# An encoder layer on one core: the first up tile's order, splits moved from GpSimd to VectorE, exponentials and inverse roots kept in PSUM, deeper gate loads

## The chip, the core and the metric

The kernel runs on one core of a Trainium2 chip. A core has five engines with a queue of instructions each: TensorE (PE, matrix products into PSUM), VectorE (DVE), ScalarE (ACT), GpSimd (POOL) and SyncE (SP, which here only issues DMA transfers; ACT issues some too). Data lies in SBUF (128 partitions) or in PSUM (banks of 128x512 fp32), and the engines wait for one another by semaphores. The metric is the device time of one execution in microseconds; lower is better. A change of less than about 0.2% can't be told from none.

## The reference

One layer of an encoder with a final norm, for 1024 prompt tokens and 256 sample tokens that share the weights, all in fp32:

```
h = rmsnorm(x);  proj = h @ w_in      # q,k,v, beta/decay inputs, gates, gMLP u/v, two branch gates
y_a = deltanet(q,k,v,...) @ w_up_a    # 4 heads, two directions, chunks with a triangular inverse
y_b = (gelu(u) * (w_s @ layernorm(gelu(v)) + b)) @ w_up_b
x  += (sigmoid(gate_a)*y_a + sigmoid(gate_b)*y_b) @ w_out
x  += softmax(q k^T) v @ w_o          # 4 heads, 256 memory tokens, q from rmsnorm(x), k/v from rmsnorm(mem)
gu  = rmsnorm(x) @ w_gate_up          # 1024 -> 2 x 2816
x  += (silu(gate) * up) @ w_down
y   = rmsnorm(x)
```

## The kernel before

**Precision.** Each fp32 operand of a large product is split into two parts: `hi`, its rounding to the fast matmul type (an ACT pass), and `lo`, the rest (a subtraction on DVE or POOL); a product is three matmuls, hi.hi, lo.hi and hi.lo. `split(hi, lo, src, eng)` (L125, L126) does both, and `eng` says who subtracts.

**Blocks.** The tokens stand as columns in three blocks, b = 0 and 1 of 512 and b = 2, the sample, of 256; the channels as 8 tiles of 128 rows. The order of stages: first norm, sv/u projections and the gMLP; q/k/v and gates with the DeltaNet heads 0 to 3 and a batch of the sample's four heads beside them; the memory projections `mem_k` and `mem_v` (770 to 880 us); the branch projections `up_b` and `up_a` (to 1040); w_out, attention, w_o; the FFN's up half (1450 to 2040) and its down half with the final norm.

**Order.** PE's order is written out by hand. Main generators issue matmuls and advance a modelled clock by their cost; side generators (norms, DeltaNet batches, loads) are resumed when that clock passes the number that they yielded, so numbers such as `ROOT`, `LAGF` and `PACEF` set where a side's instructions fall between the main ones. The other engines' order follows from the program order and a scheduler. `K.take()` returns the split of the next weight tile in a fixed list, `K.ahead()` splits the one after and requests the next load (raw weights, two buffers); with `K.lo_vector` true DVE does the subtraction of these weights, else POOL.

**Norms.** `Norm.add` squares a tile on ACT and sums on DVE (or POOL); `Norm.rest` sums over the partitions with matmuls against a column of ones (`nacc`), takes the inverse square root on DVE (`rsqrt`, an integer start at L224 and three rounds of L226, L227, L228 on tiny tiles, `nst`), spreads it with matmuls against the identity (`nst`), and scales the tiles (`nt`, L275; with `shared`, some on ACT and POOL, L270, L271).

**Memory stage.** While PE does `mem_k`, DVE computes the sample batch's triangular inverse (`W`, L721 and L724, row by row) and the end of head 3: the output `o` is scaled by an inverse root (`cw`) at L920, and PE transposes it (L121). `yb`, `ylo` are the splits of the branch inputs, `stage` and `ga`/`gb` tiles hold stored gates (`gtd`, `tbd`) that are loaded back.

**Attention.** Per chunk of 128 tokens DVE takes the negative maximum of a score bank (L1277), ACT the exponential into `e` with its sum (L1279), DVE the scaling (L1281); PE transposes `e`.

**FFN up.** The gate and up products of a tile `f` are formed from seven half products (a scheme of Strassen's kind) of the left inputs b11, b21, b22, r1, r2, t3, t4; `gate_of` and `times_up` combine the banks `pb`, `pf`, `pe`, `pa` (pool `pm`, four banks). r2, t3 and t4 of the first tile are built by DVE at the stage's start, t3 and t4 ahead of the generator's first matmul in program order. `pn` and `pn2` belong to the next tile.

Of the kernel before, what the change touches and what calls it, by code (L numbers as in the profile page):

```python
# [8 lines left out]
F32 = mybir.dt.float32  # L9
F32R = mybir.dt.float32r  # L10
# [153 lines left out]
def trunk_kernel(ctx: ExitStack, tc: tile.TileContext, a):  # L164
# [65 lines left out]
    class Norm:  # L230
# [16 lines left out]
        def rest(self, xk, wcol, sink, pace=1300, shared=(), lag=1500, ks=range(KT), inplace=False, ready=None):  # L247
# [5 lines left out]
            for c in range(nb):  # L253
                mm(pc[:, c : c + 1], self.acc[:, c * P : (c + 1) * P], one)
            st = p.tile([P, 3, 4], F32, tag="nst", name="nst", bufs=2)
            ms, y, sc = (st[:, i, :nb] for i in range(3))
# [74 lines left out]
    def sv_load(half):  # L331
        lo = svp.tile([P, 8 * 264], F32R, tag="lo", name="svl")
        hi = svp.tile([P, 8 * 264], F32R, tag="hi", name="svh")
        for i in range(2):
            sl = slice(i * 1056, (i + 1) * 1056)
            raw = K.raw()
            SY.dma_start(raw, a["w_sv"][half][:, sl])
            split(hi[:, sl], lo[:, sl], raw, V if half and i else G)
# [7 lines left out]
    SY.dma_start(cst, a["const"])  # L346
    x_h = act_tiles()
    first = K.side(norm(xp, lambda k: xs[:, k, :], NS, S_MIX, to_h(x_h, 2), 0, 0))
    sv_load(0)
    x0 = x_load(a["xT"], 0, 512, "x0")  # L350
    sv_load(1)
# [641 lines left out]
    K.lo_vector = False  # L993
# [24 lines left out]
    def load_yb():  # L1018
        for b, (t0, n) in enumerate(BLOCKS):
            hi, lo = yb_h[b]  # L1020
            for k in range(4):
                raw = staging(n)
                SY.dma_start(raw, ybd[k, :, t0 : t0 + n])
                split(hi[:, k, :], lo[:, k, :], raw, G)
                yield 2000

    def mem_k(m):
        w = K.take()
        ps = bank(pm)
        for k in range(KT):  # L1030
# [5 lines left out]
            if k == 3:  # L1036
                K.ahead()
# [4 lines left out]
    def mem_v(h):  # L1042
        pss = [bank(pm)[:, :256] for _ in range(4)]
        for i in range(2):
            w = K.take()
            for c in range(4):
# [7 lines left out]
                if c == 1:  # L1054
                    K.ahead()
# [37 lines left out]
    def load_ya():  # L1093
# [14 lines left out]
        def finish(b, k, t):  # L1108
            hi, lo = y_h[b]
            V.tensor_tensor(out=t[0], in0=t[0], in1=t[1], op=ALU.mult)  # L1110
            split(hi[:, k : k + 2, :], lo[:, k : k + 2, :], t[0], V if b else G)
# [35 lines left out]
    def merge_load():  # L1147
        if len(merged) < len(jobs):
            m, b = jobs[len(merged)]
            t0, n = BLOCKS[b]  # L1150
            ta, tb = (up.tile([P, 512], F32, tag=f"g{x}", name=f"g{x}", bufs=3)[:, :n] for x in "ab")
# [4 lines left out]
    def up_a():  # L1156
        merge_load()
# [14 lines left out]
    K.main(up_a())  # L1172
    ues.close()
# [4 lines left out]
    class OutProj:  # L1178
# [21 lines left out]
        def run(self, xsrc, scale, wcol, xpool, store, sinks=None, then=None, ready=None):  # L1200
# [23 lines left out]
            for b, (t0, n) in enumerate(BLOCKS):  # L1224
# [17 lines left out]
                else:  # L1242
                    norm_b = nms[b].rest(xk, wcol, sinks(b, x, hs), 600, inplace=True)
# [18 lines left out]
    def attend(h, qh, ql, kh, kl, vh, vl, o_h):  # L1262
        es = {}

        def scores(b, c):
# [13 lines left out]
            S.activation(e, ps, AF.Exp, bias=st[:, 0:1], accum_out=st[:, 1:2])  # L1279
            V.reciprocal(st[:, 2:3], st[:, 1:2])  # L1280
            V.tensor_scalar(out=e, in0=e, scalar1=st[:, 2:3], scalar2=None, op0=ALU.mult)  # L1281
# [215 lines left out]
    split(*gu_w[0, 2], gu_raw[0][0], V)  # L1497
# [3 lines left out]

    for k in range(4):
        parts(r2, k, r2_raw[k], V)
    for k in range(4):
        V.tensor_tensor(out=x1[:, k, :], in0=x1[:, k + 4, :], in1=x1[:, k, :], op=ALU.subtract)
        parts(t3, k, x1[:, k, :], V)
    xhs.close()
    fs = ExitStack()
    fp = fs.enter_context(pool("ffn", side="right"))
# [294 lines left out]
```

## Time and profile before

| | us |
|---|---|
| median of 3 runs (2341.19 to 2343.51) | 2341.20 |
| the profiled execution | 2346.75 |
| its span, first to last instruction | 2344.8 |
| busy in it: PE / DVE / ACT / POOL | 2245.1 / 1320.2 / 754.6 / 660.3 |
| mean granted TensorE clock | 0.986 |

In the rows of the timeline the columns are the start in us, the duration in us, the engine, the line of the program, the operation and `out<-in` with shapes; `x4` says that neighbouring rows were joined, and the bracket gives the engine's idle time before the row and what ended it. In a table of stretches each engine's busy time in the stretch stands with its number of instructions, then the granted clock, the busy share of the DMA engines and GB/s. A row of waits gives the total of one kind of wait, the number, and the longest.

### The profile page before, as it was taken

To read this page: it belongs to the slowest core of one execution; us is meant where nothing else is said; L and a number is where in the kernel's file an instruction comes from. 1 tells how busy PE (TensorE), PEld (TensorE's weight loads), DVE (VectorE), ACT (ScalarE), POOL (GpSimd) and SP (SyncE) were. 2 spreads that over 40 slices of the span, in tenths; PEclk is the share of its full clock that TensorE was granted. 3 is DMA by queue.
4 is the path that set the end of the run, shared out by engine and by line. 5 is a ranking of instruction groups with operands and counts; after the bars stand their busy time and mean duration, and the time that the engine had idled before them with its cause. 6 is when DMAs were issued, how large, how long until landed. Compare 5 with 4: busy or idle time off the path is not lost. (4 is left out here: it accounts for less than half of the span.)

```text
span 2344.8 us, 32531 instructions
## 1 busy us (share of the span) xinstructions
PE 2245.1 (96%) x12592; PEld 1952.6 (83%) x12592; DVE 1320.2 (56%) x2716; ACT 754.6 (32%) x1391; POOL 660.3 (28%) x409
## 2 busy tenths in 40 slices
PE   5999999999999899999999999899999999999997
PEld 4988888888888788878888888788888888888886
DVE  7758688887967844464534547522322323656445
ACT  4433242433423433122234423332222223312113
POOL 3010000000001522123221321666666665212114
PEclk9999999999999999999999999999999999999998
DMA  4221312223243535763221431121211221723202
GB/s 147 102 86 65 113 53 91 76 66 89 65 133 94 164 107 203 236 227 115 74 93 59 156 132 63 67 87 66 69 62 66 78 72 44 255 99 102 81 10 90
DMA packets 170309, 237.83 MB, mean 101 GB/s; under 512 B 71386, under 2 KB 98858, under 8 KB 170154
## 3 DMA queue, kind: packets, MB, share of 16 engines
q1 hardware_dynamic: 150314, 206.65, 27.3%
q10 hardware_dynamic: 19840, 29.11, 3.4%
q8 instruction: 98, 1.61, 0.3%
q14 instruction: 57, 0.47, 0.1%
HBM read 166.20 MB, written 69.51 MB: 101 GB/s over the span
## 5 line engine op out<-in xcount | busy, mean ns | idle before, releaser
L108 PE MATMUL bank<-hi,whi 128*128 128x512 f32 (+1 forms) x2144 | 766.4, 357 | 10.7 <-DVE g L1548 8.8
L108 PE MATMUL bank<-hi,wlo 128*128 128x512 f32 (+1 forms) x2144 | 750.1, 350 | 0.0
L108 PE MATMUL bank<-lo,whi 128*128 128x512 f32 (+1 forms) x2144 | 750.1, 350 | 0.0
L108 PEld LDWEIGHTS bank<-hi,whi 128*128 128x128 f32 x2144 | 407.3, 190 | 60.6 <-issue 9.6
L108 PEld LDWEIGHTS bank<-hi,wlo 128*128 128x128 f32 x2144 | 406.4, 190 | 54.3
L108 PEld LDWEIGHTS bank<-lo,whi 128*128 128x128 f32 x2144 | 407.7, 190 | 48.5 <-issue 0.2
L126 POOL TENSOR_TENSOR wlo<-raw,whi 128x1024 fp32r<-128x1024 f32 x97 | 244.8, 2526 | 584.9 <-ACT whi L125 537.6
L125 ACT ACTIVATE whi<-raw 128x1024 fp32r<-128x1024 f32 x151 | 159.2, 1058 | 355.8 <-PE bank L108 275.3
L108 PE MATMUL bank<-ghi,whi 128*128 128x512 f32 (+1 forms) x528 | 189.3, 358 | 1.2 <-DVE x L1682 1.2
L108 PE MATMUL bank<-ghi,wlo 128*128 128x512 f32 (+1 forms) x528 | 188.5, 357 | 0.8 <-DVE wlo L126 0.8
L108 PE MATMUL bank<-glo,whi 128*128 128x512 f32 (+1 forms) x528 | 187.4, 355 | 0.0
L1682 DVE SCALAR_TENSOR_TENSOR x<-bank,x 128x512 f32<-128x512 f32 (+1 forms) x192 | 112.5, 598 | 132.6 <-PE bank L108 126.4
L126 POOL TENSOR_TENSOR wlo<-room,whi 128x1024 fp32r<-128x1024 f32 x42 | 101.7, 2422 | 126.7 <-ACT whi L125 126.7
L108 PEld LDWEIGHTS bank<-ghi,whi 128*128 128x128 f32 x528 | 99.4, 188 | 17.0 <-DVE x L1682 2.1
L108 PEld LDWEIGHTS bank<-ghi,wlo 128*128 128x128 f32 x528 | 99.3, 188 | 16.6 <-DVE wlo L126 1.3
L108 PEld LDWEIGHTS bank<-glo,whi 128*128 128x128 f32 x528 | 99.5, 188 | 15.1
L126 POOL TENSOR_TENSOR glo<-graw,ghi 128x1280 fp32r<-128x1280 f32 x13 | 46.4, 3588 | 203.3 <-ACT ghi L125 203.3
L1645 DVE TENSOR_TENSOR room<-room,bank 128x512 f32<-128x512 f32 x21 | 14.4, 688 | 143.0 <-ACT room L1528 143.0
L721 DVE TENSOR_TENSOR W<-W,UT 128x2 f32<-128x2 f32 (+30 forms) x155 | 84.7, 546 | 14.3 <-DMA W<-in_eye 9.5
L125 ACT ACTIVATE whi<-room 128x1024 fp32r<-128x1024 f32 x42 | 44.6, 1061 | 137.3 <-PE bank L108 137.3
L575 DVE SCALAR_TENSOR_TENSOR acc<-craw,sm,acc 128x510 f32<-128x510 f32 (+1 forms) x96 | 72.5, 756 | 23.1 <-ACT acc L573 22.0
L1548 DVE TENSOR_TENSOR g<-room,bank 128x512 f32<-128x512 f32 x42 | 28.9, 687 | 97.5 <-PE bank L108 97.5
(303 smaller groups left out, 3875.0 us busy)
## 6 DMA issues: line engine op xcount, KB each, us to landing
raw<-in_w_gu SPq DMA_DIRECT2D x44, 512.0 KB, 3.8
graw<-gd SPq DMA_DIRECT2D x20, 640.0 KB, 5.3
gd<-t SPq DMA_DIRECT2D x44, 256.0 KB, 2.4
raw<-in_w_dn SPq DMA_DIRECT2D x22, 512.0 KB, 4.0
raw<-in_w_g SPq DMA_DIRECT2D x20, 512.0 KB, 3.4
gtd<-gs ACTq DMA_DIRECT2D x32, 256.0 KB, 2.0
raw<-in_w_qkv SPq DMA_DIRECT2D x12, 512.0 KB, 3.6
x<-in_xT SPq DMA_DIRECT2D x10, 512.0 KB, 8.7
```

The source lines that it names most:

```text
L108: self.nc.tensor.matmul(out, l, r, start=start, stop=stop, skip_group_check=more)
L125: self.nc.scalar.activation(hi, src, AF.Copy)
L126: (eng or self.nc.vector).tensor_tensor(out=lo, in0=src, in1=f32(hi), op=ALU.subtract)
L575: V.scalar_tensor_tensor(out=dst, in0=src, scalar=wj, in1=dst, op0=ALU.mult, op1=ALU.add)
L721: V.tensor_tensor(out=t3, in0=u3[:, i:, c:].rearrange("p j c -> p c j"), in1=XL[:, 32 * i + i : 32 * i + 32].unsqueeze(1).to_broadcast([P, ...
L1548: V.tensor_tensor(out=g, in0=p, in1=ps, op=ALU.add)
L1645: V.tensor_tensor(out=c22, in0=u3, in1=pe, op=ALU.add)
L1682: V.scalar_tensor_tensor(out=x2[b][:, m, :], in0=ps, scalar=0.5, in1=x2[b][:, m, :], op0=ALU.mult, op1=ALU.add)
```

## The change

Eight edits, which the diff shows in the order of the file:

1. `rsqrt` in a norm works in the norm's PSUM bank (columns 4 to 11) rather than in SBUF; only its result lies in SBUF.
2. At the start, the first norm squares pairs of tiles (512 columns) and sums both halves with the matmuls; the constants are loaded in two parts around the first two sv weights; of each sv half DVE splits the second part.
3. `K.lo_vector` stays true through the memory and branch projections, and the yb and ylo splits go to DVE: no split of these stages is left on POOL. `K.ahead()` comes at the first step of a tile rather than the fourth or second.
4. `ROOT` for head 3 goes from 10000 to 16000, which moves the transposes of `o` 27 rows later in PE's order.
5. `up_a` loads its gates three jobs ahead, in six buffers, rather than one ahead in three.
6. The exponential stays in its PSUM bank and is scaled from there.
7. The first up tile: t3 and t4 are made inside the generator, behind the first matmul groups; `pn2` stands ahead of the t3 product; the next tile's raw weights are loaded in two parts at two places; the norm of block 1 has a slower pace (`PACE1`).
8. The final norm: lags 3500, 2800 and 1500 for the blocks in place of 4500, pace 500 in place of 700, and the sums of tiles from `FADD` on are on DVE (6 and 4 rather than 8 and 8; block 2's were there).

```diff
-        def rest(self, xk, wcol, sink, pace=1300, shared=(), lag=1500, ks=range(KT), inplace=False, ready=None):
+        def rest(self, xk, wcol, sink, pace=1300, shared=(), lag=1500, ks=range(KT), inplace=False, ready=None, halves=1):
...
-                mm(pc[:, c : c + 1], self.acc[:, c * P : (c + 1) * P], one)
-            st = p.tile([P, 3, 4], F32, tag="nst", name="nst", bufs=2)
-            ms, y, sc = (st[:, i, :nb] for i in range(3))
+                for i in range(halves):
+                    mm(pc[:, c : c + 1], self.acc[:, i * n + c * P : i * n + (c + 1) * P], one, i == 0, i == halves - 1)
+            y = p.tile([P, 4], F32, tag="nst", name="nst", bufs=2)[:, :nb]
+            ms, sc = pc[:, 4 : 4 + nb], pc[:, 8 : 8 + nb]
...
-    def sv_load(half):
+    def sv_raw(half):
+        raws = [K.raw() for _ in range(2)]
+        for i, raw in enumerate(raws):
+            SY.dma_start(raw, a["w_sv"][half][:, i * 1056 : (i + 1) * 1056])
+        return raws
+    def sv_split(half, raws):
...
-        for i in range(2):
+        for i, raw in enumerate(raws):
...
-            raw = K.raw()
-            SY.dma_start(raw, a["w_sv"][half][:, sl])
-            split(hi[:, sl], lo[:, sl], raw, V if half and i else G)
+            split(hi[:, sl], lo[:, sl], raw, V if i else G)
...
-    SY.dma_start(cst, a["const"])
+    SY.dma_start(cst[:, C_BD:], a["const"][:, C_BD:])
+    sv_raw0 = sv_raw(0)
+    SY.dma_start(cst[:, :C_BD], a["const"][:, :C_BD])
...
-    first = K.side(norm(xp, lambda k: xs[:, k, :], NS, S_MIX, to_h(x_h, 2), 0, 0))
-    sv_load(0)
+    def first_norm():
+        nm = Norm(xp, 512)
+        for k in range(0, KT, 2):
+            nm.add(xs[:, k : k + 2, :].rearrange("p k t -> p (k t)"))
+        nm.n = NS
+        yield from nm.rest(lambda k: xs[:, k, :], S_MIX, to_h(x_h, 2), 0, lag=0, halves=2)
+    first = K.side(first_norm())
+    sv_split(0, sv_raw0)
...
-    sv_load(1)
+    sv_split(1, sv_raw(1))
...
-    K.lo_vector = False
...
-                split(hi[:, k, :], lo[:, k, :], raw, G)
+                split(hi[:, k, :], lo[:, k, :], raw, V)
...
-            if k == 3:
+            if k == 0:
...
-                if c == 1:
+                if c == 0:
...
-            split(hi[:, k : k + 2, :], lo[:, k : k + 2, :], t[0], V if b else G)
+            split(hi[:, k : k + 2, :], lo[:, k : k + 2, :], t[0], V)
...
-            ta, tb = (up.tile([P, 512], F32, tag=f"g{x}", name=f"g{x}", bufs=3)[:, :n] for x in "ab")
+            ta, tb = (up.tile([P, 512], F32, tag=f"g{x}", name=f"g{x}", bufs=6)[:, :n] for x in "ab")
...
-        merge_load()
+        for _ in range(3):
+            merge_load()
...
+    K.lo_vector = False
...
-                    norm_b = nms[b].rest(xk, wcol, sinks(b, x, hs), 600, inplace=True)
+                    norm_b = nms[b].rest(xk, wcol, sinks(b, x, hs), (600, PACE1)[b], inplace=True)
...
-            S.activation(e, ps, AF.Exp, bias=st[:, 0:1], accum_out=st[:, 1:2])
+            S.activation(ps, ps, AF.Exp, bias=st[:, 0:1], accum_out=st[:, 1:2])
...
-            V.tensor_scalar(out=e, in0=e, scalar1=st[:, 2:3], scalar2=None, op0=ALU.mult)
+            V.tensor_scalar(out=e, in0=ps, scalar1=st[:, 2:3], scalar2=None, op0=ALU.mult)
...
-    split(*gu_w[0, 2], gu_raw[0][0], V)
...
+    split(*gu_w[0, 2], gu_raw[0][0], V)
...
-    for k in range(4):
-        V.tensor_tensor(out=x1[:, k, :], in0=x1[:, k + 4, :], in1=x1[:, k, :], op=ALU.subtract)
-        parts(t3, k, x1[:, k, :], V)
-    xhs.close()
...
-    fp = fs.enter_context(pool("ffn", side="right"))
-    t4 = [fp.tile([P, 4, 512], F32R, tag=f"t4{i}", name=f"t4{i}") for i in "hl"]
-    for k in range(4):
-        V.scalar_tensor_tensor(out=x0[:, k + 4, :], in0=r2_raw[k], scalar=-1.0, in1=x0[:, k + 4, :], op0=ALU.mult, op1=ALU.subtract)
-        parts(t4, k, x0[:, k + 4, :], V)
-    split(*gu_w[0, 3], gu_raw[0][1], V)
-    room = x0p.tile([P, KT, 512], F32, tag="x0", name="room")
+    t4 = []
+    def make_t3():
+        for k in range(4):
+            V.tensor_tensor(out=x1[:, k, :], in0=x1[:, k + 4, :], in1=x1[:, k, :], op=ALU.subtract)
+            parts(t3, k, x1[:, k, :], V)
+        xhs.close()
+    def make_t4():
+        nonlocal fp
+        fp = fs.enter_context(pool("ffn", side="right"))
+        t4.extend(fp.tile([P, 4, 512], F32R, tag=f"t4{i}", name=f"t4{i}") for i in "hl")
+        for k in range(4):
+            V.scalar_tensor_tensor(out=x0[:, k + 4, :], in0=r2_raw[k], scalar=-1.0, in1=x0[:, k + 4, :], op0=ALU.mult, op1=ALU.subtract)
+            parts(t4, k, x0[:, k + 4, :], V)
+    def make_room():
+        nonlocal room, c22
+        room = x0p.tile([P, KT, 512], F32, tag="x0", name="room")
+        c22 = room[:, 7, :]
+    fp = room = c22 = None
...
-    c22 = room[:, 7, :]
...
-        gu_load(1, wp)
+        raw = K.raw()[:, :1024]
+        SY.dma_start(raw, a["w_gu"][1])
+        gu_raw[1] = [raw]
...
+        make_t3()
...
+        gu_gate(1)
...
-        gu_gate(1)
...
+        make_t4()
+        split(*gu_w[0, 3], gu_raw[0][1], V)
+        raw = K.raw()[:, :1024]
+        SY.dma_start(raw, a["w_gu"][NFF + 1])
+        gu_raw[1].append(raw)
+        make_room()
...
+        pn2 = bank(pm)
+        first_out.extend((pn, pn2))
+        yield from gu_mm(pn2, gu_w[1, 0], 1, b21, True)
...
-        pn2 = bank(pm)
-        first_out.extend((pn, pn2))
-        yield from gu_mm(pn2, gu_w[1, 0], 1, b21, True)
...
-                nm.add(x2[b][:, m, :], G if b < 2 else V)
+                nm.add(x2[b][:, m, :], G if m < FADD[b] else V)
...
-            K.side(nm.rest(lambda k, b=b: x2[b][:, k, :], S_FIN, sink, PACEF, SHARED[b], LAGF))
+            K.side(nm.rest(lambda k, b=b: x2[b][:, k, :], S_FIN, sink, PACEF, SHARED[b], LAGF[b]))
...
-TAIL, ROOT, FIRST_EXP = 3000, (2500, 2500, 2500, 10000, 2500), 3500
+TAIL, ROOT, FIRST_EXP = 3000, (2500, 2500, 2500, 16000, 2500), 3500
...
-LAG0, LAGF, PACEF = 7500, 4500, 700
+PACE1 = 1900
+LAG0, LAGF, PACEF = 7500, (3500, 2800, 1500), 500
+FADD = (6, 4, 0)
```

In the memory stage, DVE's order around the scaling of head 3's `o` (`W` rows of the sample's inverse, `cw` rows of the inverse root), before:

```order
L721 TENSOR_TENSOR W<-W,UT_7429 128x288
L228 SCALAR_TENSOR_TENSOR cw<-cw 128x8
L724 TENSOR_REDUCE W<-W 128x12
L920 TENSOR_TENSOR o<-o,cw 128x1024
L721 TENSOR_TENSOR W<-W,UT_7429 128x300
L724 TENSOR_REDUCE W<-W 128x12
```

and after (L737 and L740 are the former L721 and L724, L936 the former L920):

```order
L737 TENSOR_TENSOR W<-W,UT_7420 128x162
L228 SCALAR_TENSOR_TENSOR cw<-cw 128x8
L740 TENSOR_REDUCE W<-W 128x9
L936 TENSOR_TENSOR o<-o,cw 128x1024
L737 TENSOR_TENSOR W<-W,UT_7420 128x171
L126 TENSOR_TENSOR wlo<-raw,whi 128x1024
L740 TENSOR_REDUCE W<-W 128x9
L126 TENSOR_TENSOR yb_7486<-stage,yb_7486 128x256
L737 TENSOR_TENSOR W<-W,UT_7420 128x200
L126 TENSOR_TENSOR yb_7485<-stage,yb_7485 128x512
```

`o` moved ahead of the step of width 171, where it stood behind the one of width 288, and weight and yb splits stand between the steps.

At the start of the FFN, DVE's order, before (x_12586 and x_12585 are the tiles from which t3 and t4 are made, L1548 the sum in `gate_of`):

```order
L126 TENSOR_TENSOR t3l<-x_12586,t3h 128x512 x3
L1505 TENSOR_TENSOR x_12586<-x_12586 128x512
L1512 SCALAR_TENSOR_TENSOR x_12585<-bank,x_12585 128x512 x3
L126 TENSOR_TENSOR t3l<-x_12586,t3h 128x512
L1512 SCALAR_TENSOR_TENSOR x_12585<-bank,x_12585 128x512
L126 TENSOR_TENSOR wlo<-raw,whi 128x1024
L126 TENSOR_TENSOR t4l<-x_12585,t4h 128x512 x4
L1548 TENSOR_TENSOR g<-copies,bank 128x512
L1594 TENSOR_TENSOR copies<-copies,bank 128x512
L1543 SCALAR_TENSOR_TENSOR t<-t,g 128x512
```

and after (L1526 and L1535 are the former L1505 and L1512, L1574 the former L1548):

```order
L1574 TENSOR_TENSOR g<-copies,bank 128x512
L1526 TENSOR_TENSOR x_12577<-x_12577 128x512 x2
L1569 SCALAR_TENSOR_TENSOR t<-t,g 128x512
L126 TENSOR_TENSOR t3l<-x_12577,t3h 128x512 x2
L1526 TENSOR_TENSOR x_12577<-x_12577 128x512 x2
L1535 SCALAR_TENSOR_TENSOR x_12576<-bank,x_12576 128x512
L126 TENSOR_TENSOR t3l<-x_12577,t3h 128x512 x2
L258 TENSOR_SCALAR bank<-bank 128x2
L1535 SCALAR_TENSOR_TENSOR x_12576<-bank,x_12576 128x512
L224 TENSOR_SCALAR nst<-bank 128x2
L126 TENSOR_TENSOR t4l<-x_12576,t4h 128x512
L226 SCALAR_TENSOR_TENSOR bank<-nst,bank 128x2
```

The gate's sum moved ahead of t3 and t4; the inverse root of the sample's norm (L258, L224, L226) stands between their splits.

At the end, DVE's order around the last norm's inverse root (x_17533 or x_17524 is block 1, x_17534 or x_17525 block 2), before:

```order
L244 TENSOR_TENSOR nacc<-nacc,nsq 128x256
L257 TENSOR_SCALAR nst<-bank 128x2
L224 TENSOR_SCALAR nst<-nst 128x2
L226 SCALAR_TENSOR_TENSOR nst<-nst 128x2
L275 SCALAR_TENSOR_TENSOR x_17533<-x_17533,sm,bank 128x512 x4
L227 TENSOR_TENSOR nst<-nst 128x2
L228 SCALAR_TENSOR_TENSOR nst<-nst 128x2
```

and after (L276 is the former L275, L1717 the former L1682):

```order
L228 SCALAR_TENSOR_TENSOR nst<-bank,nst 128x4
L276 SCALAR_TENSOR_TENSOR x_17524<-x_17524,sm,bank 128x512 x2
L1717 SCALAR_TENSOR_TENSOR x_17525<-bank,x_17525 128x256
L276 SCALAR_TENSOR_TENSOR x_17524<-x_17524,sm,bank 128x512
L1717 SCALAR_TENSOR_TENSOR x_17525<-bank,x_17525 128x256
L244 TENSOR_TENSOR nacc<-nacc,nsq 128x256
L276 SCALAR_TENSOR_TENSOR x_17524<-x_17524,sm,bank 128x512
L244 TENSOR_TENSOR nacc<-nacc,nsq 128x256
L258 TENSOR_SCALAR bank<-bank 128x2
L224 TENSOR_SCALAR nst<-bank 128x2
L226 SCALAR_TENSOR_TENSOR bank<-nst,bank 128x2
```

The four scalings of block 1 stood inside the inverse root of block 2 and stand ahead of it now, between the last tiles of block 2.

## The prediction

> **What bounds the kernel.** I read the busy shares of the page first, then a table of stretches, then the chain of waits of TensorE (PE), and last the timeline around each long wait.
>
> ```profile
> PE 2245.1 (96%) x12592; PEld 1952.6 (83%) x12592; DVE 1320.2 (56%) x2716; ACT 754.6 (32%) x1391; POOL 660.3 (28%) x409
> core 0: us, PE busy (x) PEld busy (x) DVE busy (x) ACT busy (x) POOL busy (x), PEclk, DMA share, GB/s
> 0.00:60.00 60.00, 33.93 (x201) 30.27 (x202) 46.52 (x100) 28.61 (x58) 21.04 (x17) 0.94 0.45 153
> 770.00:850.00 80.00, 67.71 (x367) 58.43 (x367) 58.97 (x102) 31.01 (x64) 36.93 (x22) 0.94 0.50 153
> 850.00:935.00 85.00, 79.15 (x576) 74.41 (x575) 33.16 (x66) 30.09 (x78) 26.43 (x14) 0.97 0.46 159
> 935.00:1040.00 105.00, 99.68 (x497) 83.93 (x496) 63.32 (x93) 21.73 (x32) 16.78 (x7) 0.98 0.68 214
> 1445.00:1485.00 40.00, 28.92 (x135) 23.68 (x135) 36.21 (x63) 18.94 (x32) 8.62 (x6) 0.87 0.20 66
> 1485.00:2038.00 553.00, 553.00 (x2940) 477.87 (x2939) 172.05 (x230) 164.55 (x226) 327.53 (x170) 1.00 0.25 84
> 2325.00:2345.00 20.00, 5.31 (x39) 4.76 (x37) 12.12 (x37) 2.74 (x6) 7.03 (x7) 0.68 0.43 158
> ```
>
> PE is busy 2245.1 of 2344.8 us, so at most 99.7 us of waiting is there to win, plus what matmuls lose while the granted clock (PEclk) is below 1. The FFN's middle (1485 to 2038) has no waiting: nothing done there counts. The idle time sits in the start (26.1 us), the memory projections (12.3), the branch projections (5.9 and 5.3), the start of the FFN (11.1) and the end (14.7), and the change touches each. What happens in them repeats one picture:
>
> ```profile
> 10.34 1.01 PE L108 MATMUL bank<-cst,nacc 128*128 128x1 f32 x4 [10.34 <-DVE nacc L244]
> 11.39 0.16 DVE L257 TENSOR_SCALAR nst<-bank 128x2 f32<-128x2 f32 x1 [1.11 <-PE bank L108]
> 11.85 4.77 POOL L126 TENSOR_TENSOR svl<-raw,svh 128x1056 fp32r<-128x1056 f32 x2 [11.41 <-ACT svh L125]
> 11.98 2.29 DVE L227 TENSOR_TENSOR nst<-nst 128x2 f32<-128x2 f32 x1
> 14.31 2.33 DVE L228 SCALAR_TENSOR_TENSOR nst<-nst 128x2 f32<-128x2 f32 x1
> 16.68 0.16 DVE L226 SCALAR_TENSOR_TENSOR nst<-nst 128x2 f32<-128x2 f32 x1
> 17.87 1.22 PE L108 MATMUL bank<-cst,nst 128*128 128x128 f32 x4 [6.52 <-DVE nst L228]
> ...
> 32.70 1.25 DVE L126 TENSOR_TENSOR svl<-raw,svh 128x1056 fp32r<-128x1056 f32 x1
> 37.64 2.26 DVE L227 TENSOR_TENSOR nst<-nst 128x4 f32<-128x4 f32 x1
> 39.93 2.27 DVE L228 SCALAR_TENSOR_TENSOR nst<-nst 128x4 f32<-128x4 f32 x1
> 43.74 1.13 PE L108 MATMUL bank<-cst,nst 128*128 128x128 f32 x8 [2.70 <-DVE nst L228]
> ```
>
> A two-element step of the inverse square root takes 0.16 us, but 2.3 us while GpSimd (POOL) runs a split: the first ends at 14.27, when the first of POOL's two splits does, the second at 16.64, with the other. Both have all tensor operands in SBUF. PE waits for the result.
>
> **Start (gain 6 us, 3 to 11).** The scratch of the inverse square root moves into its PSUM bank, so that each of its ten steps has a PSUM operand. The first norm loses two stalls: 2.29 + 2.33 - 2 x 0.16 = 4.30 us. The added cost on that path is half of the first sv split, which now stands on VectorE (DVE) ahead of the scaled tiles: 1.25 us by the row at 32.70. It may also have to wait for POOL's half, which begins a microsecond before it. Fewer, wider squares give some 0.5 us. Net 3.5. The constant table comes in two loads, five columns first and the rest behind the sv weights; it is one more request on SP (0.4 us of issue) and only the five columns are needed by the sum's matmuls, so I cost it at nothing: the x tiles behind it are wanted ten microseconds later, and if that cover fails it costs the 0.4. In the second norm 2.26 + 2.27 - 0.32 = 4.2 us of stalls go, of which PE waited 2.70; with the neighbouring sums on DVE now in between I take 2.5. Sum 6. Lower end: the sv split starts late and eats the first gain but for 0.5. Upper end: the later short waits before 60 us shrink too and the clock, 0.94 here, holds.
>
> A rule of the Trainium skill speaks against PSUM operands: "VectorE: DVE Perf Modes" (section "The TRN2 errata") charges a PSUM source 120 cycles where it charges SBUF 58, by which ten steps would cost an estimated 0.65 us more for each norm, and the start would give 4.7 us instead of 6. The trace does not agree: the step at 11.39, which reads PSUM, took 0.16 us, as the one at 16.68 in SBUF did.
>
> **Memory projections (gain 6 us, 0 to 10).**
>
> ```profile
> 798.25 2.40 POOL L126 TENSOR_TENSOR wlo<-raw,whi 128x1024 fp32r<-128x1024 f32 x1
> 798.48 2.21 DVE L224 TENSOR_SCALAR cw<-cw 128x8 int32<-128x8 int32 x1
> 811.18 1.97 PE L121 MATMUL bank<-cst,o 128*128 128x128 f32 x8 [5.17 <-DVE o L920]
> 837.65 1.06 ACT L125 ACTIVATE whi<-raw 128x1024 fp32r<-128x1024 f32 x1 [7.86 <-DMA raw<-in_w_v]
> 838.76 0.39 PE L108 MATMUL bank<-whi,mhi 128*128 128x256 f32 x1 [2.27 <-ACT whi L125]
> 841.18 0.58 PE L108 MATMUL bank<-wlo,mhi 128*128 128x256 f32 x1 [1.92 <-POOL wlo L126]
> ```
>
> POOL's weight splits (2.40 us) stop the serial chain of products for the sample's inverse on DVE; with them goes `o`, for which PE waits 5.17 us. Now DVE does the splits. By the POOL program's rows 26 weight splits, 12 of yb and two of ylo move. A split of 128x1056 on DVE took 1.25 us, so 128x1024 is an estimated 1.21, and by width 26 x 1.21 + 8 x 0.61 + 4 x 0.30 + 2 x 1.21 = 40 us go onto DVE between 770 and 1040. DVE has 21 + 52 + 42 = 115 us of idle time there, before a stall is taken off. `o` is normalised six inverse steps earlier in DVE's order and its transposes stand 27 rows later in PE's, so I count the 5.17 as gone. The split behind the ACT half shortens by 2.40 - 1.21 = 1.2 us at 841.18. The load behind the wait at 838.76 stands in SP's queue after the writes of the inverse; the loads are now requested earlier, so one more weight stands ahead of them, but PE also arrives earlier. Together 5.17 + 1.2 - 0.4 for `W`'s reload, which now stands behind one more weight = 6. Lower end 0: PE only reaches that load sooner. Upper end: all of 5.17 + 2.27 + 1.92 and some clock.
>
> **Branch projections (gain 7.5 us, 3 to 9).**
>
> ```profile
> 930.19 2.33 POOL L126 TENSOR_TENSOR ylo<-t,yhi 128x1024 fp32r<-128x1024 f32 x1
> 930.30 3.31 DVE L1110 TENSOR_TENSOR t<-t,t 128x1024 f32<-128x1024 f32 x1 [1.73 <-DMA t<-sgd]
> 934.00 1.22 PE L108 MATMUL bank<-yb,whi 128*128 128x512 f32 x2 [3.68 <-DVE stage L1087]
> ...
> PE bank L108 <- DVE ga L1168: 5.3, 5, 2.4
> ...
> 1015.66 0.69 DVE L1168 SCALAR_TENSOR_TENSOR ga<-ga,bank 128x512 f32<-128x512 f32 x1 [3.32 <-DMA ga<-gtd]
> ```
>
> At 930.30 a product of 128x1024 takes 3.31 us under POOL's ylo; without it some 1.2 (the estimate for a split of that shape), so 2.1 of PE's 3.68 go; I take 2.5, since POOL's next splits go as well. Later PE waits 5.3 us in five waits for a gate whose load was late. Six buffers instead of three, with three loads ahead, send each load two jobs earlier. The longest that DVE sat there was 3.32, and two jobs of lead are longer than that, since a job's DVE passes alone are three of 0.69. I take 5 of 5.3. On SP a load now stands behind other gate loads and the next weight. Lower end: the loads only queue behind one another.
>
> **Attention (1.5, 0 to 3) and its PSUM operand.**
>
> ```profile
> 1190.85 1.89 DVE L1281 TENSOR_SCALAR e<-e,st 128x256 f32<-128x256 f32 x1
> 1192.79 1.79 PE L121 MATMUL bank<-cst,e 128*128 128x128 f32 x6 [1.68 <-DVE e L1281]
> 1192.84 0.35 DVE L1281 TENSOR_SCALAR e<-e,st 128x256 f32<-128x256 f32 x1
> ```
>
> Normalising takes 0.35 us free and 1.89 under POOL; from PSUM the stall of 1.54 goes. A 128x256 pass with a PSUM operand may take longer than 0.35; even at 0.7 each the forty add 14 us to an engine half idle here. The bank is held until then rather than until the exponential; I cost that at nothing, because four banks rotate, and up to 1.5 us if that cover fails. "VectorE: DVE Perf Modes" of the Trainium skill (section "Why PSUM operands drop a tier") has the PSUM form lose the double rate, which points the same way as my 0.7.
>
> **First up tile (1, -3 to 3).**
>
> ```profile
> 1472.79 2.48 DVE L126 TENSOR_TENSOR t4l<-x,t4h 128x512 fp32r<-128x512 f32 x4
> 1476.01 0.77 PE L108 MATMUL bank<-hi,whi 128*128 128x512 f32 x1 [8.77 <-DVE g L1548]
> ```
>
> PE waits 8.77 us for the gate that frees a bank, behind all of t3 and t4 on DVE. Now g stands ahead of them. But what PE meets next stands behind them: the sample norm's sum needs a pq bank that the first t4 pass reads, its broadcast the inverse square root among the t4 splits, and pn's third matmul the gate's weight split on POOL, which follows t4's ACT halves. DVE is busy 36.21 of 40 us here, and nothing is taken off it but stalls. So the wait turns into two or three of about the same sum. I keep 1.
>
> **End (3.5, 1.5 to 5).**
>
> ```profile
> 2332.03 2.71 DVE L275 SCALAR_TENSOR_TENSOR x<-x,sm,bank 128x512 f32<-128x512 f32 x4
> 2334.67 1.12 DVE L227 TENSOR_TENSOR nst<-nst 128x2 f32<-128x2 f32 x1
> 2337.22 1.23 PE L108 MATMUL bank<-cst,nst 128*128 128x128 f32 x4 [6.75 <-DVE nst L228]
> ```
>
> The last norm's inverse square root is held by four scalings of the block before (2.71 us) and a stall (0.96). Both leave the chain: 3.67. Six sums of squares move from POOL to DVE (0.7 us each by a scaling's 2.71 / 4), beside matmuls of block 1, so at nothing; without that cover they cost 4. The scalings stand earlier, because block 1's last sums are done sooner and its lag is shorter; if its broadcast comes too early PE waits there by about as much as it now waits for it. I take 3.5.
>
> **Sum.** 6 + 6 + 7.5 + 1.5 + 1 + 3.5 = 25.5 us. The profiled execution took 2346.75 (span 2344.8), 5.55 above the median of 2341.2; from its own time the sum gives 2321.2, from the median 2315.7, and I predict 2316. All low ends give 4.5, all high ends 41.
>
> **Rivals.** (1) The loads bind: the memory stage gives 0 and gates 2.5 rather than 7.5; 14.5 us are left, 2327. The 7.86 us wait of ACT for a weight speaks for it; that the DMA engines are busy 0.50 of that stretch, against. (2) Slower: DVE runs its queue in order, and a moved split waits for its weight with the inverse's chain behind it, where POOL waited alone. A wait like ACT's costs up to 7.86 us; it must outweigh 25.5 + 4.7, so four such on the chain, giving about 2347. DVE's idle time speaks against. (3) The gains only change their place, as at the first up tile: within 4.7 us of 2341. (4) The clock: removed gaps lift it. At 0.94 over 80 us up to 4.8 us are lost, at 0.87 over 40 us 5.2, at 0.94 over 60 us 3.6; all of it back gives 2316 - 13.6 = 2302. "TensorE: Matmul & The Clock Gate" of the Trainium skill (Part 1) has the clock go down after an idle window of 3.4 us, which is this rival's mechanism.
>
> **Chances.** Forecast 0.60, (1) 0.17, (2) 0.08, (3) 0.06, (4) 0.09. Forecast, (1) and (4) lie between 2300 and 2334, which leaves out (2), (3) and a little of (1). A change within 0.2% (4.7 us) can't be told from none: faster 0.86, same 0.06, slower 0.08.
>
> **What would show it.** After: no inverse-root step over 0.3 us in the norms; PE's wait at L920's place gone and none like it before 850; no wait for ga over 1 us; the wait of 8.77 replaced by several at the sample norm; the last wait under 4 us. A DVE weight split preceded by a long wait for whi, with PE idle behind it, would make the forecast wrong.

## The result and the profile after

| | before | after |
|---|---|---|
| median, us | 2342.36 (2341.19 to 2344.13, 4 runs) | 2327.16 (2322.34 to 2329.20, 4 runs) |
| profiled execution, its span | 2346.75, 2344.8 | 2328.12, 2326.3 |
| mean granted clock | 0.986 | 0.989 |

The ratio is 0.9932 with a 95% interval of 0.9914 to 0.9949: 15.2 us faster, where 25.5 were forecast. The busy shares of the page, and the table of stretches for the same work as in the rows of before (the borders are moved with PE's matmuls):

```profile
PE 2241.6 (96%) x12596; PEld 1947.7 (84%) x12596; DVE 1313.0 (56%) x2759; ACT 754.1 (32%) x1387; POOL 567.6 (24%) x362
core 0: us, PE busy (x) PEld busy (x) DVE busy (x) ACT busy (x) POOL busy (x), PEclk, DMA share, GB/s
0.00:53.10 53.10, 33.97 (x204) 30.58 (x205) 38.56 (x97) 28.41 (x54) 19.16 (x16) 0.95 0.51 171
276.00:296.00 20.00, 17.85 (x81) 15.36 (x80) 8.45 (x12) 4.45 (x9) 0.04 (x1) 0.74 0.48 95
770.20:836.00 65.80, 63.39 (x367) 55.17 (x366) 50.57 (x120) 30.33 (x63) 0.00 (x0) 1.00 0.59 171
836.00:917.70 81.70, 77.30 (x576) 72.64 (x576) 41.76 (x79) 31.05 (x79) 3.10 (x4) 1.00 0.49 168
917.70:1017.60 99.90, 96.99 (x496) 82.13 (x495) 67.25 (x103) 23.76 (x36) 5.20 (x2) 1.00 0.74 236
1420.00:1465.30 45.30, 33.48 (x144) 26.82 (x143) 36.27 (x71) 20.35 (x38) 7.82 (x5) 0.81 0.18 58
2303.60:2326.30 22.70, 8.13 (x57) 7.38 (x55) 13.47 (x43) 4.40 (x10) 7.24 (x7) 0.73 0.38 139
```

Where the two traces have the same PE instruction, its start can be compared. Between such landmarks (times of before) the change won or lost as follows; the column "second trace" is the changed kernel in its second measurement, `again` below:

| stretch of before, us | gain, us | second trace | predicted |
|---|---|---|---|
| 0 to 60 | 6.8 | 8.2 | 6 |
| 60 to 770 | -7.0 | -5.7 | 0 |
| 770 to 850, memory projections | 14.1 | 14.1 | 6 |
| 850 to 1040, branch projections | 8.4 | 8.6 | 7.5 |
| 1040 to 1445, attention among it | 2.6 | 2.8 | 1.5 |
| 1445 to 2300, start of the FFN among it | -5.9 | -3.1 | 1 |
| 2300 to the end | -0.5 | -0.1 | 3.5 |
| sum of the traces (spans 2344.8 to 2326.3 and 2320.0) | 18.5 | 24.8 | 25.5 |

Two rows with losses are the news: the start's gain is spent before the memory stage begins, and the new order of the first up tile costs. The stall itself, on which most terms rest, went as foreseen. The first norm, in the timeline of after:

```profile
10.62 2.41 POOL L126 TENSOR_TENSOR svl<-raw,svh 128x1056 fp32r<-128x1056 f32 x1 [10.18 <-ACT svh L125]
11.51 0.17 DVE L227 TENSOR_TENSOR bank<-bank,nst 128x2 f32<-128x2 f32 x1
11.71 0.16 DVE L228 SCALAR_TENSOR_TENSOR nst<-bank,nst 128x2 f32<-128x2 f32 x1
12.98 1.26 DVE L126 TENSOR_TENSOR svl<-raw,svh 128x1056 fp32r<-128x1056 f32 x1
13.12 1.22 PE L108 MATMUL bank<-cst,nst 128*128 128x128 f32 x4 [2.24 <-DVE nst L228]
```

The steps at 11.51 and 11.71 stand inside POOL's split (10.62 to 13.03) and take 0.17 and 0.16 us, where they took 2.29 and 2.33 before. The DVE split with two SBUF operands begins at 12.98, as that split of POOL ends. PE's wait for the norm is 2.24 us instead of 6.52. That only one SBUF operand is left is what the Trainium skill names as the condition ("SBUF — State Buffer", section "Who interferes with whom": a DVE instruction with two SBUF inputs contends with a GpSimd instruction that reads SBUF); the rows agree. Two inputs were not needed for a stall, though: in the prediction's rows of before, the `cw` step at 798.48 and the `e` pass at 1190.85 read one tensor each, from SBUF, and took 2.21 and 1.89 us under POOL. What the quick steps of after have in common is an operand in PSUM.

### The profile page after: what moved, and what is told of

Read it like the earlier page. It is cut to its first block, busy times and chain, and to the rows that moved or that the text cites. A ratio compares the mean times of both kernels' runs of the same rounds, so it can differ in the third digit from the quotient of the medians.

```text
span 2326.3 us, 32511 instructions
## 1 busy us (share of the span) xinstructions
PE 2241.6 (96%) x12596; PEld 1947.7 (84%) x12596; DVE 1313.0 (56%) x2759; ACT 754.1 (32%) x1387; POOL 567.6 (24%) x362
## 4 chain that ended last, share of the span: by engine, by line
PE 46%; DVE 2%; DMA 1%; issue 1%; POOL 1%; ACT 0%; POOLq 0%; ACTq 0%; DVEq 0%; SPq 0%
PE bank L108 45%; DMA raw<-in_w_dn 0%; DMA kraw<-vd 0%; PE bank L121 0%; POOL x L272 0%; POOL wlo L126 0%; DVE wlo L126 0%; POOL kv L126 0%; DMA kraw<-kd 0%; DMA raw<-in_w_gu 0%; DVE x L1717 0%; DMA raw<-gd 0%; DVE t4l L126 0%; DVE x L1526 0%; DVE r2l L126 0%
## 5 line engine op out<-in xcount | busy, mean ns | idle before, releaser
L126 POOL TENSOR_TENSOR wlo<-raw,whi 128x1024 fp32r<-128x1024 f32 x71 | 180.5, 2545 | 439.1 <-ACT whi L125 435.9
L1717 DVE SCALAR_TENSOR_TENSOR x<-bank,x 128x512 f32<-128x512 f32 (+1 forms) x192 | 112.4, 598 | 125.3 <-PE bank L108 120.0
L126 DVE TENSOR_TENSOR wlo<-raw,whi 128x1024 fp32r<-128x1024 f32 x80 | 106.6, 1338 | 31.0 <-ACT whi L125 30.9
L1574 DVE TENSOR_TENSOR g<-room,bank 128x512 f32<-128x512 f32 x42 | 28.9, 688 | 103.4 <-PE bank L108 103.4
```

The source lines that it names most:

```text
L126: (eng or self.nc.vector).tensor_tensor(out=lo, in0=src, in1=f32(hi), op=ALU.subtract)
L1574: V.tensor_tensor(out=g, in0=p, in1=ps, op=ALU.add)
L1717: V.scalar_tensor_tensor(out=x2[b][:, m, :], in0=ps, scalar=0.5, in1=x2[b][:, m, :], op0=ALU.mult, op1=ALU.add)
```

## The experiments

Every kernel was timed beside the kernel before, whose medians there were 2341.26 to 2341.71. Differences between kernels are given against a second measurement of the changed kernel, unaltered:

> The changed kernel once more. Theory (the clock drops in stretches that follow short waits, at places that differ from run to run): 2322 to 2330 us, the same waits in the same places (6.7 us at the sample norm's sum, 4.5 at the last norm's), but the 10.3 us at half clock from 283 us on need not come again; without it the span is some 5 us shorter. Rival (the half clock there belongs to the 2.15 us wait for vw): it comes again, of the same length.

Measured: 2323.10 us (2321.75 to 2326.12), ratio 0.9925 (0.9912 to 0.9937), 4 us under the first measurement. Medians of one kernel can thus differ by 4 us between two measurements, and differences of that size or less, below, say little without the traces. The stretch of half clock near 283 us came again, though shorter (6.8 us instead of 10.2), and so did the waits at the FFN's start, so they belong to the kernel.

**Where the start's gain goes.** Parts 1 and 2 undone (norm scratch in SBUF for every norm, old start):

```diff
-            y = p.tile([P, 4], F32, tag="nst", name="nst", bufs=2)[:, :nb]
-            ms, sc = pc[:, 4 : 4 + nb], pc[:, 8 : 8 + nb]
+            st = p.tile([P, 3, 4], F32, tag="nst", name="nst", bufs=2)
+            ms, y, sc = (st[:, i, :nb] for i in range(3))
...
-    sv_raw0 = sv_raw(0)
```

> The changed kernel with the first norm, the sv splits, the constant's load and the inverse roots of the norms (scratch in SBUF) as before. Theory (the start's gain of 7 us is spent at 283 us, where PE waits for DVE's chain of products for head 0's inverse, and on clock stretches): within 3 us of the changed kernel, 2325 to 2330 us, and PE ahead of the kernel before by no more than 1 us at 450. Rival (the start's gain lasts): 2333 to 2335 us.

Measured: 2324.46 us (2322.33 to 2327.61), 0.9931 (0.9919 to 0.9944), within noise of the changed kernel (+1.4). The traces tell why. At 100 us the changed kernel (its second trace) is 8.4 us ahead of before and this one 1.6; from 300 to 650 both are 1.4 to 1.6 ahead. Of the 6.9 us that it loses on the way, 2.1 go between 100 and 150, 1.5 of them where 3.4 us of half clock follow PE's wait of 2.39 us for `gm` (at 124.56 in its times). The other 4.7, and 6.6 in the first trace, go at one place, where PE forms sums of squares of head 0's keys (`gs`) behind DVE's `vw`. Timeline of before, then of after:

```profile
285.36 1.28 DVE L747 TENSOR_TENSOR vw<-bank,cw 128x512 f32<-128x512 f32 x2
286.19 1.02 PE L108 MATMUL bank<-cst,gs 128*128 128x1 f32 x8 [0.35 <-DVE vw L747]
287.85 0.40 PE L108 MATMUL bank<-hi,whi 128*128 128x512 f32 x1
```

```profile
282.11 1.28 DVE L763 TENSOR_TENSOR vw<-bank,cw 128x512 f32<-128x512 f32 x2
282.94 1.57 PE L108 MATMUL bank<-cst,gs 128*128 128x1 f32 x8 [2.15 <-DVE vw L763]
285.80 0.63 PE L108 MATMUL bank<-hi,whi 128*128 128x512 f32 x1
287.08 1.70 PE L108 MATMUL bank<-cst,gs 128*128 128x1 f32 x8
```

PE arrives 5.05 us earlier (280.79 instead of 285.84, the start of the row less its wait), but DVE's inverse, a serial chain ahead of `vw`, ends only 3.25 us earlier. So PE waits 2.15 us instead of 0.35, and then runs at half clock for 10.2 us: a matmul of 128x512 takes 0.63 us instead of 0.40, and the stretch 276 to 296 has a granted clock of 0.74. The wait and the slow stretch cost 6.6 us (4.7 in the second trace, with a wait of 1.91 and 6.8 us of half clock). The counter-test puts that group of sums later among PE's matmuls; what follows it in the same head shifts with it, so PE's order differs from the changed kernel's up to about 750 us:

```diff
-            yield SQ
+            yield SQ + (4000 if bi == 0 and hf == 0 else 0)
```

> The changed kernel with the first four sums of squares of head 0 (the matmuls that wait for vw at 283 us) 18 matmuls later in PE's order. Theory (the 1.3 to 2.2 us wait for vw there and the 6.8 to 10 us at half clock behind it eat the start's gain): both go, 4 to 6 us gained, about 2318 us. Rival (the chain of products is late for everything behind it, or the small matmuls lower the clock by themselves): the wait returns at UT or U, or the half clock stays, 2322 to 2324 us.

Measured: 2315.02 us (2313.68 to 2316.62), 0.9888 (0.9875 to 0.9902), 8.1 us under the changed kernel. Its timeline, and its table of stretches for the same place:

```profile
279.94 1.29 DVE L763 TENSOR_TENSOR vw<-bank,cw 128x512 f32<-128x512 f32 x2
283.25 0.95 PE L108 MATMUL bank<-cst,gs 128*128 128x1 f32 x8
284.38 0.39 PE L108 MATMUL bank<-lo,whi 128*128 128x512 f32 x1
```

```profile
274.00:294.00 20.00, 20.00 (x122) 17.74 (x121) 12.01 (x18) 8.29 (x14) 0.29 (x2) 1.00 0.48 97
```

No wait and full clock. Measured by the matmul columns that PE has done, this kernel leads before by 6.5 us ahead of this place and by 7.1 at 300 us, where the changed kernel's second trace leads by 1.5. That what was left of the start's gain was spent here is therefore shown, not only argued. The 8.1 us are not all from this place: at 775 us the leads are 11.2 and 2.5, so about 3 us more were won behind it, part of them at 453 us, where a stretch of 3.4 us at half clock is gone; no run takes that part from the other shifts in the order.

**The first up tile.** Part 7 undone (t3 and t4 ahead of the generator again, old places of `pn2`, the loads and the pace):

```diff
+    for k in range(4):
+        V.tensor_tensor(out=x1[:, k, :], in0=x1[:, k + 4, :], in1=x1[:, k, :], op=ALU.subtract)
+        parts(t3, k, x1[:, k, :], V)
...
-        make_t3()
...
-        make_t4()
```

> The changed kernel with the first up tile's order, the split weight loads and the norm's pace of before. Theory (the new order costs about 6 us, since the sample norm's sum now stands inside the second group and waits 6.7 us for a bank that t4 reads): about 2321 us, one wait of some 8 us in that stage. Rival (the order gains the predicted 1 us and the stage's loss is the clock): about 2328 us.

Measured: 2317.77 us (2313.23 to 2323.05), 0.9904 (0.9888 to 0.9921): 5.3 us faster than with part 7. The intervals of the two overlap a little, so the traces have to tell: between 1445 and 1500 (times of before) the changed kernel loses 6.1 and 3.3 us in its two traces, and this kernel gains 0.2. PE's longest waits there, of after and of this kernel:

```profile
1442.51 0.98 PE L108 MATMUL bank<-cst,nacc 128*128 128x1 f32 x4 [6.70 <-DVE x L1535]
1450.13 0.71 PE L108 MATMUL bank<-cst,nst 128*128 128x128 f32 x4 [1.34 <-DVE nst L228]
1452.45 0.50 PE L108 MATMUL bank<-hi,whi 128*128 128x512 f32 x1 [0.91 <-ACT whi L125]
1454.96 0.80 PE L108 MATMUL bank<-hi,wlo 128*128 128x512 f32 x1 [1.78 <-POOL wlo L126]
1467.20 0.50 PE L108 MATMUL bank<-t4h,whi 128*128 128x512 f32 x1 [1.47 <-ACT copies L1556]
```

```profile
1447.87 0.77 PE L108 MATMUL bank<-hi,whi 128*128 128x512 f32 x1 [8.77 <-DVE g L1565]
```

One wait of 8.77 us against five that sum to 12.20; with the shorter ones PE idles 10.7 us here and 13.7 in after. The clock is halved in every one of these traces, twice here (3.4 and 6.8 us), twice in after (10.2 and 6.8) and once in its second trace (6.8), so it is the waits that cost each time, and the clock varies. The longest wait is the sample norm's sum (`nacc`), which needs a bank that the first t4 pass (L1535) reads. A second run only puts that norm later:

```diff
-LAGS, FIRST_W = 13500, 9000
+LAGS, FIRST_W = 18000, 9000
```

> The changed kernel with LAGS 18000 in place of 13500: the sample norm's sum and its spreading stand 21 and 24 matmuls later in PE's order, in pn and pn2; nothing else moves on PE. Theory (the early sum is what costs): the 6.7 us wait goes and no wait over 3 us replaces it, 4 to 6 us gained, about 2322 us. Rival (DVE is full there and bounds the stage in any order): the wait comes back at pn, at the spreading or at t4, and the time stays at 2326 to 2328 us.

Measured: 2318.88 us (2314.64 to 2325.06), 0.9904 (0.9888 to 0.9920), 4.2 under the changed kernel; its trace loses 0.2 us between 1445 and 1500. PE's longest waits in it:

```profile
1441.83 0.80 PE L108 MATMUL bank<-hi,wlo 128*128 128x512 f32 x1 [2.43 <-POOL wlo L126]
1444.27 0.99 PE L108 MATMUL bank<-cst,nacc 128*128 128x1 f32 x4 [1.64 <-DVE x L1535]
1452.17 0.71 PE L108 MATMUL bank<-cst,nst 128*128 128x128 f32 x4 [1.86 <-DVE nst L228]
1459.02 0.50 PE L108 MATMUL bank<-t4h,whi 128*128 128x512 f32 x1 [2.00 <-ACT copies L1556]
```

6.70 became 1.64, and 2.43 of POOL stands ahead of it: most of the loss was where the norm fell in PE's order, and DVE's work in this stage still sets the rest.

**Memory and branch projections.** Part 3 undone (`mem_before`: the splits back on POOL, the loads' old places), the loads' places alone (`ahead_before`), part 4 alone (`root_before`), part 5 alone (`gates_before`):

```diff
+    K.lo_vector = False
...
-                split(hi[:, k, :], lo[:, k, :], raw, V)
+                split(hi[:, k, :], lo[:, k, :], raw, G)
...
-            if k == 0:
+            if k == 3:
```

> The changed kernel with the weight, yb and ylo splits of the memory and branch projections back on POOL and K.ahead at the places of before; ROOT stays at 16000. Theory (POOL's splits stop DVE's instructions with two SBUF operands, and that is most of the 20 us that these stages gained): 8 to 12 us slower than the changed kernel's 2323, about 2333 us, with inverse-root steps of over 2 us on DVE between 770 and 830. Rival (ROOT's move of the transposes is what gained): at most 3 us slower, about 2326 us.

Measured: 2336.24 us (2333.82 to 2340.81), 0.9982 (0.9973 to 0.9990), 13.1 slower than the changed kernel: the largest part of the whole gain. Its timeline:

```profile
792.54 2.43 POOL L126 TENSOR_TENSOR wlo<-raw,whi 128x1024 fp32r<-128x1024 f32 x1
793.12 2.08 DVE L737 TENSOR_TENSOR W<-W,UT 128x162 f32<-128x162 f32 x1
...
826.78 0.60 ACT L1055 ACTIVATE stage<-bank 128x512 f32<-128x512 f32 x1 [11.44 <-DMA vsd<-UT]
828.37 0.58 PE L108 MATMUL bank<-whi,mhi 128*128 128x256 f32 x1 [5.99 <-ACT whi L125]
830.86 0.58 PE L108 MATMUL bank<-wlo,mhi 128*128 128x256 f32 x1 [1.69 <-POOL wlo L126]
```

A row of the inverse takes 2.08 us under POOL's split; in the changed kernel that step takes 0.45. ACT then idles 11.44 us: its queue stands at the second write of `o`, which it issues only at 826.33, when a write of that inverse (`usd`) has landed, and the next weight's `whi` pass is queued behind that on ACT: PE waits 5.99. Against the changed kernel's second trace it falls back 6.4 us between 785 and 800, 6.2 to 815 and 3.4 to 824.

```diff
-            if k == 0:
+            if k == 3:
...
-                if c == 0:
+                if c == 1:
```

> The changed kernel with K.ahead at its places of before (fourth step of a mem_k tile, second of mem_v), the splits still on DVE. Theory (the engine that splits is what counts): at most 3 us slower than 2323, about 2325 us; the weight behind the writes of the inverse is late by 1 to 3 us. Rival (the earlier requests are what gained): 8 us or more slower, since the waits of 6 us for a weight at 828 us, which the kernel with both undone shows, come back.

Measured: 2325.06 us (2320.16 to 2326.62), 0.9924 (0.9911 to 0.9937): +2.0, no difference that can be told. It is the engine of the splits that counts.

```diff
-TAIL, ROOT, FIRST_EXP = 3000, (2500, 2500, 2500, 16000, 2500), 3500
+TAIL, ROOT, FIRST_EXP = 3000, (2500, 2500, 2500, 10000, 2500), 3500
```

> The changed kernel with ROOT 10000 for head 3: the transposes of o stand 27 rows earlier in PE's order, as before. Theory (o comes early enough once DVE isn't stopped): the wait for o returns with 1 to 3 us, 2324 to 2326 us. Rival (the place of the transposes is what gained): the wait of 5 us and the half clock behind it return, 2331 us.

Measured: 2323.01 us (2322.45 to 2326.78), 0.9926 (0.9913 to 0.9940): nothing. The wait of 5.17 us for `o` does not come back with the old order, nor in `mem_before` with the new; either edit removes it by itself.

```diff
-... name=f"g{x}", bufs=6)[:, :n] for x in "ab")
+... name=f"g{x}", bufs=3)[:, :n] for x in "ab")
...
-        for _ in range(3):
-            merge_load()
+        merge_load()
```

> The changed kernel with the gate loads of up_a one job ahead in three buffers, as before. Theory (the deeper loads took the waits for ga): the waits of 1 to 2.4 us for ga come back, 4 to 6 us slower than 2323, about 2328 us. Rival (the waits went because POOL no longer stops DVE there): at most 1 us slower.

Measured: 2322.80 us (2317.29 to 2323.82), 0.9913 (0.9898 to 0.9928): nothing, where 4 to 6 us were expected. DVE waits for the gates' loads again, but PE never waits for `ga`. Row of the waits of this kernel, then of the groups of `mem_before` and of the changed kernel's second trace (the sum in which the gated terms are combined):

```profile
DVE ga L1183 <- DMA ga<-gtd: 5.8, 6, 1.9
```

```profile
L1186 DVE TENSOR_TENSOR ga<-ga,gb 128x512 f32<-128x512 f32 (+1 forms) x24 | 23.8, 992 | 0.8
```

```profile
L1185 DVE TENSOR_TENSOR ga<-ga,gb 128x512 f32<-128x512 f32 (+1 forms) x24 | 14.5, 603 | 0.8
```

Before, two things made DVE late here: loads (8.9 us of waiting) and POOL's splits, under which that sum took 992 ns in the mean instead of 603. `gates_before` has the first without the second, `mem_before` the second without the first, and in neither does PE wait for `ga`. Each edit alone is enough; only the two together made PE wait.

The other long wait of the branch projections, for `stage`, was only spread. Rows of PE's waits, before and after:

```profile
PE bank L108 <- DVE stage L1087: 3.9, 2, 3.7
```

```profile
PE bank L108 <- DVE stage L1102: 4.5, 5, 1.6
```

**Attention.** Part 6 undone:

```diff
-            S.activation(ps, ps, AF.Exp, bias=st[:, 0:1], accum_out=st[:, 1:2])
+            S.activation(e, ps, AF.Exp, bias=st[:, 0:1], accum_out=st[:, 1:2])
...
-            V.tensor_scalar(out=e, in0=ps, scalar1=st[:, 2:3], scalar2=None, op0=ALU.mult)
+            V.tensor_scalar(out=e, in0=e, scalar1=st[:, 2:3], scalar2=None, op0=ALU.mult)
```

> The changed kernel with the exponential and its scaling in SBUF as before. Theory (POOL's splits stop the scaling at the first head alone): 1 to 3 us slower than 2323, all of it between 1155 and 1175 us, steps of 1.9 to 2.1 us on DVE there. Rival (the bank that is held longer costs as much): no difference.

Measured: 2326.06 us (2323.18 to 2332.26), 0.9937 (0.9921 to 0.9953): +3.0, hardly above the noise, but the trace has the place. This kernel, then after:

```profile
1165.44 2.34 POOL L126 TENSOR_TENSOR kv<-kraw,kv 128x1024 fp32r<-128x1024 f32 x1 [2.82 <-ACT kv L125]
1166.05 1.89 DVE L1298 TENSOR_SCALAR e<-e,st 128x256 f32<-128x256 f32 x1
1167.99 1.23 PE L121 MATMUL bank<-cst,e 128*128 128x128 f32 x6 [1.68 <-DVE e L1298]
```

```profile
1168.37 2.36 POOL L126 TENSOR_TENSOR kv<-kraw,kv 128x1024 fp32r<-128x1024 f32 x1 [3.00 <-ACT kv L125]
1168.98 0.48 DVE L1298 TENSOR_SCALAR e<-bank,st 128x256 f32<-128x256 f32 x1
```

From PSUM the pass takes 0.48 us under a split, from SBUF 1.89 (0.35 when free). The old form falls back 2.7 us around it, most of that by 3.4 us of half clock; such a stretch shows here in some traces of the new form too. PE's waiting hardly changed. The 1.68 at the transposes is gone, but the bank of the scores is now held until the scaling, and PE waits for it (row of the waits of after):

```profile
PE bank L108 <- DVE e L1298: 2.5, 2, 1.6
```

With 1.05 us left at the transposes, the new form's waits there sum to 3.58 us, those of the old form (0.93, 0.91 and 1.68) to 3.52.

**The end.** Block 1's last norm later, so that the last sums of block 2 come before its broadcast:

```diff
-LAG0, LAGF, PACEF = 7500, (3500, 2800, 1500), 500
+LAG0, LAGF, PACEF = 7500, (3500, 6500, 1500), 500
```

> The changed kernel with LAGF 6500 rather than 2800 for block 1: the scalings of block 1 stand behind the last sums and behind both inverse roots on DVE. Theory (the 4.5 us wait for the last sum comes from the scalings that stand ahead of it): that wait falls below 1.5 us and the wait for the spreading stays near 3, some 2 us gained, 2321 us. Rival (the end is bound by the scalings and POOL's products wherever they stand): 2323 to 2325 us.

Measured: 2323.29 us (2320.30 to 2325.40), 0.9922 (0.9909 to 0.9936): nothing, though PE's waits shrink. The timeline of after, then the last lines of this kernel's chain (start, us, what):

```profile
2310.03 5.15 POOL L272 TENSOR_TENSOR x<-x,nacc 128x512 f32<-128x512 f32 x4 [13.93 <-ACT nacc L268]
2312.63 1.42 DVE L244 TENSOR_TENSOR nacc<-nacc,nsq 128x256 f32<-128x256 f32 x1
2315.61 0.99 PE L108 MATMUL bank<-cst,nacc 128*128 128x1 f32 x4 [4.50 <-DVE nacc L244]
2318.84 1.22 PE L108 MATMUL bank<-cst,nst 128*128 128x128 f32 x4 [2.24 <-DVE nst L228]
```

```profile
2311.94 1.27 POOL x L272
2313.21 1.23 POOLq L1836
2314.44 4.50 POOL x L272 x5
```

In the first PE waits 4.50 and 2.24 us. In the second it waits 1.52 and 1.13 and ends 11.5 us before the end instead of 6.3, because POOL's products of the last tiles (seven, 7.00 us) and DVE's nine scalings (4.68) then stand one behind the other. PE's last wait was no bound of its own.

**Both losses mended.** Part 7 undone and the sums of head 0 put later, as above:

> The changed kernel with the first up tile as before and the first sums of squares of head 0 18 matmuls later: the two losses taken out together. Theory (they lie in different stages and add): 2323 - 5 - 8 = 2310 us. Rival (PE's lead is spent at a later wait, so the two share one gain): 2314 to 2316 us.

Measured: 2309.36 us (2306.47 to 2310.39), 0.9856 (0.9841 to 0.9872). The two mendings add (5.3 + 8.1 = 13.4 against 13.7), and this version is the fastest of all, 32 us under the kernel before.

## Why the prediction was right, and where not

- **The mechanism held where it was about stalls.** No step of a norm's inverse root takes over 0.17 us; the waits at `o` and for `ga` are gone; the 8.77 was replaced by several waits at the sample norm, all as the prediction's last part asked. The total is partly luck: memory gained 8.1 more than its term, which covers half of what start, first up tile and end fell short by.
- **Start (6): 6.8 by 60 us, but it did not reach the end.** The step that failed is the sum's rule that a gain at the start is a gain of the kernel. I read the later stretch's idle time as fixed; it had a wait of 0.35 us, DVE's inverse nearly as late as PE, and DVE did not move forward as far as PE did. About 2 us had already gone before 150 us, most of them to half clock. This is rival (3), gains that only change their place, for one term alone.
- **Memory projections (6): 14.1, the mis-sized term.** PE's idle time fell from 12.29 to 2.41 us, that is 9.9, and its busy time by 4.3, since the clock went from 0.94 to 1.00. I counted 5.17 + 1.2 and left 2.27 and the clock to the upper end, though the half clock stood at the same waits (6.8 us from 810.0 on, 3.4 from 840.7 on); and the W rows' stalls delayed more than `o`. Rival (2), DVE's queue in order, had no such wait: the longest that PE waited for a DVE weight split is 1.1.
- **Branch projections (7.5): 8.4, the right size in part by luck.** I summed 7.5 us of waits. PE's idle time fell by 3.9 us (11.2 to 7.3), its busy time by 4.5, since two stretches of half clock (3.4 and 6.8 us) are gone. The waits for `ga` went as said, but those for `stage`, where I took 2.5 off, did not shrink in sum, although the product that POOL's ylo had held takes 1.22 us instead of 3.31. That deeper loads bring 5 of it holds only against the old kernel: beside part 3 they bring nothing, as `gates_before` shows, and part 3 alone would do.
- **Attention (1.5): 2.6, but not by the wait.** The pass from PSUM takes 0.48 us, under the 0.7 that I bounded it by. The step that failed is the bank that I cost at nothing because four rotate: PE's idle time between 1040 and 1445 went from 5.2 to 5.9 us, and the gain is clock (6.8 us of half clock at 1192 are gone), which isn't steady at this place.
- **First up tile (1): -3 to -6.** I named the three waits that would come, with their causes, and then summed them to the old wait because DVE is as busy as before. The five sum to 12.20 instead of 8.77, and in the first trace 10.2 and 6.8 us of half clock stand there, where before had 3.4 and 6.8. An engine's busy time does not give the sum of the waits on it; each place where PE meets DVE's queue had to be walked for itself.
- **End (3.5): -0.5.** The inverse root left POOL's stalls as said and the last wait fell to 2.24, but a wait of 4.50 stands ahead of it: the sums ahead of it fell under POOL's products (1.42 instead of 0.42), and `last_norm` shows that the products themselves bound the end.
- **Rival (1), the loads bind, has nearly the measured time (2327), and not its reason:** memory gained more than forecast, not nothing. Rival (4), the clock, happened in part: half clock went from 63.6 to 49.7 us in sum (40.5 in the second trace), gone in the memory and branch stages but for 3.4 us in the second trace, new at 126 and 283. "TensorE: Matmul & The Clock Gate" of the Trainium skill (Part 1) has an idle window of about 3.4 us put it down; here it went down behind waits of 1.0 to 2.4 us, so a wait need not be that long.

## What to carry to other kernels

A gain ahead of a serial chain on another engine lasts only until PE meets that chain: before you book it, look downstream for the short waits (0.35 us here), which say that a second engine is just as late. A PSUM bank that is held longer, as in the attention here, can move a wait to the bank's next user. Moving a POOL split away from DVE work that reads only SBUF can be worth more than the wait it is read from, since the chain behind, the load behind that and the clock come with it. When two edits cure one wait, undo each alone before you credit either.

## What the hardware showed beyond that

The half clock behind the wait at `vw` is steady and goes by steps. In ten traces of kernels with the early start and the sums at their place, waits there of 1.03 to 1.91 us (seven traces) were followed by 6.8 us of half clock, waits of 2.08 to 2.15 (three) by 10.2; 0.35 and 0.37 (before and `start_before`) by none. Behind the wait stand matmuls of a single column (128x1, 1.0 to 1.7 us for eight), and again 2.5 us later. In `vw_later` the same matmuls without a wait cost no clock. Whether the single columns prolong the slow stretch was not tried apart. The length of a wait alone does not decide: PE waits 2.39 to 2.41 us for `gm` between 121 and 133 us in all fourteen traces, and 3.4 us of half clock follow in the twelve with the early start, none in before and `start_before`. In each trace all changes of the clock lie on one grid of 3.41 us. In the twelve at least 2.1 us of that wait fall into one interval of the grid, in the two a line of the grid divides it and at most 1.7 fall into one. That the place on the grid decides fits these traces but was not tried. A norm step on two or four elements takes 0.15 to 0.17 us with a PSUM operand as with SBUF alone.
